# A two-layer hybrid diffusion backbone on one Trainium2 core: the start, the phase boundaries and the filler work of the mixers are rearranged

## The chip, the cores and the metric

The kernel runs on one core of a Trainium2 chip. A core has a matmul engine (TensorE, in the profile PE, with its weight loads as PEld), a vector engine (VectorE, DVE), an engine for activations and copies (ScalarE, ACT), a general one (GpSimd, POOL) and one that issues DMAs (SyncE, SP). Each works through its own instructions in order, and they wait for one another by semaphores. The metric is the device time of one execution, in microseconds (us). The kernel before took 2119.14 us in the median of three runs (2117.68 to 2120.08).

## The reference, cut to what matters

Everything is float32. There are 256 latent tokens and 256 context tokens of width 1024 and two layers. In each layer nine modulation vectors of width 1024 (shift, scale and gate for each of three sublayers) come from `silu(c)` for latent tokens and from `silu(c_ctx)` for context tokens:

```python
sc, scc = jax.nn.silu(c), jax.nn.silu(c_ctx)
for l in range(DEPTH):
    mod = (sc @ w_ada[l] + b_ada[l]).reshape(B, 1, N_MOD, D)
    mod_c = (scc @ w_ada[l] + b_ada[l]).reshape(1, 1, N_MOD, D)
    h = ffn_half_step(h, g_ffn1[l], mod[:, :, 0], mod[:, :, 1], mod[:, :, 2], ...)
    u = modulate(rmsnorm(h, g_mix[l]), mod[:, :, 3], mod[:, :, 4])
    y, yc = token_mixer(u, uc, ...)
    h = h + mod[:, :, 5] * y
    h = ffn_half_step(h, g_ffn2[l], mod[:, :, 6], mod[:, :, 7], mod[:, :, 8], ...)

def ffn_half_step(h, g, shift, scale, gate, w1, w3, w2):
    u = modulate(rmsnorm(h, g), shift, scale)
    return h + 0.5 * gate * ((jax.nn.silu(u @ w1) * (u @ w3)) @ w2)
```

The context stream goes through the same steps with `mod_c`, but not behind the mixer of the last layer. The token mixer projects u into latent attention (8 heads), a pooling mixer, a gated linear attention (GLA, 4 heads) and three sigmoid gates of width 1024. It projects each branch back to 1024, multiplies it by its gate, sums the three and applies `w_out`.

## The kernel before

**Tiles.** Activations lie transposed: 128 features on the partitions, 512 tokens on the free axis (256 latent, then 256 context), so a vector of width 1024 is eight tiles (k = 0 to 7). `self.h` is the residual in that form. Tiles of 128 x 512 come from a pool of 70 slots, PSUM tiles from a pool of eight.

**Products.** A float32 product is done as three matmuls of rounded parts (`mm3`, L238 to L240): each operand is split into a high part, written by ScalarE (`whi`, `uhi`, `hi`, L190), and a low part, the difference, written by VectorE (`wlo` on L202, `ulo` on L521 or L560).

**Weights.** `Weights` holds a list of all weight loads, written down in a first pass over the program. `run_ahead` loads the next units into four raw buffers and splits them while at most `room` slots are held. `room` is set by phase (ROOM_1 and ROOM_2 in the first FFN, ROOM_FFN, ROOM_MIX).

**Order.** The program is written as one stream. A planner then places each engine's instructions by their place in that stream (or a priority lowered by `high_priority(offset=-LATE)`) and by its own estimate of when operands are ready. `behind(i, others)` adds an order without a wait for data: i is placed after the others.

**Phases.** ffn(0,1), mixer(0), ffn(0,2), ffn(1,1), mixer(1), ffn(1,2). Behind a phase the mean of squares of the new residual is taken (`ms`, L508), `rstd` from it, then `ut`, `uhi`, `ulo`, and the next phase's products start. In the last FFN only 256 tokens are left, and its output is made by tokens: `ht` is the residual turned, `gt` the gate spread over rows.

**Modulation.** A slab (l, j) is 512 of the 9216 columns of `w_ada[l]`, in eight row blocks. Slab i = j // 2 is the half j % 2 of modulation vector i. `ada` has two forms. On TensorE (L370), a slab's eight products go to four column groups of one PSUM tile, are copied (`adaev`), turned (L384), reduced and added to the bias. The four first slabs (0, 2, 1, 3 of layer 0) are done so from rows loaded at the start, as are the two of EDGE, whose rows come over POOL's queue: (0,17) at the head of ffn(0,2) and (1,17) at the head of ffn(1,2). On VectorE, all others: per row block two multiply-adds (L401, L403), at the end two transposes, two reductions (L418, L419) and one small matmul (L424). `ada_all` is a generator over all slabs, and `adas(n)` advances it by n steps. On VectorE a step also earns half a credit. ADA holds the steps given per phase.

**Start.** `setup` loads x and ctx by tokens, then the rows of slabs 0 and 2, three units of weights, and the rows of slabs 1 and 3. ScalarE takes the squares, `xr` is x normalized, `turned` turns it into `hr`, and `residual` turns x into `h`. `first_norm` makes u from `hr`, and `dense_first` multiplies six output tiles by the k of half 0 (k below 4, slabs 0 and 2), then by those of half 1, calling one entry of `steps` after each k.

**Mixer.** `filler` yields pieces of projection work (gates, pooling inputs, GLA inputs, branch products), while `attend` and `gla` are the latency-bound chains. For each step of a chain FILL gives credit, and each whole credit advances the filler by one piece. `gate(j)` is one gate tile of 24 matmuls. While the filler waits for another chain it yields without work.

Of the kernel before, what the change touches and what calls it, by code (L numbers as in the profile page):

```python
# [15 lines left out]
P = 128  # L16
# [22 lines left out]
NHALF, NSLOT, ROOM_FFN, ROOM_MIX, RAWS = 4, 70, 20, 20, 4  # L39
RAWS_ADA = 3  # L40
ROOM_1, ROOM_2, LAST = 16, 36, 4
# [4 lines left out]
GATES = (2, 12)  # L46
EDGE = {(1, 17): (1, 2), (0, 17): (0, 2)}
# [94 lines left out]
class Net:  # L142
    def __init__(self, nc, a, cst, msk, vecs, wa2, out, pools, w, wada):
# [6 lines left out]
        self.ahead = self.seconds = None  # L150
# [83 lines left out]
    def mm3(self, out, wts, x, start, stop):  # L234

        (wh, wl), (xh, xl) = wts, x
        mm = self.nc.tensor.matmul
        mm(out, wh, xh, start=start, stop=False)  # L238
        mm(out, wh, xl, start=False, stop=False)  # L239
        mm(out, wl, xh, start=False, stop=stop)  # L240
# [12 lines left out]
    def setup(self):  # L253
# [39 lines left out]
        self.act(out=self.csil[:, :, 0:2], in_=self.vec[0][:, V_C:V_C + 16].rearrange("p (s k) -> p k s", s=2), func=AF.Silu)  # L293
# [5 lines left out]
        for j in range(4):  # L299
# [5 lines left out]
            self.act(out=f, in_=f, func=AF.Exp, scale=-0.5)  # L305
# [5 lines left out]
        self.residual(range(4), [normed])  # L311
        self.hr = []
        for k in range(KD):
            t = self.slot(name="hr")
            if k % 2:
                self.act(out=t, in_=self.turned(xr, k), func=AF.Copy)
            else:
                nc.vector.tensor_copy(t, self.turned(xr, k))
            self.hr.append(t)

    def turned(self, x, k):
        ps = self.ps()
        for j in range(4):
            self.nc.tensor.transpose(ps[:, j * P:(j + 1) * P], x[j][k // 4][:, (k % 4) * P:(k % 4 + 1) * P], self.ident)
        return ps

    def residual(self, ks, others=()):
        for k in ks:
            if k < 4:
                i = self.nc.vector.tensor_copy(self.h[:, k, :], self.turned(self.xin, k))  # L330
                if self.tc:
                    self.behind(i, others)
            else:
                self.act(out=self.h[:, k, :], in_=self.turned(self.xin, k), func=AF.Copy)
# [24 lines left out]
    def ada(self, l, j):  # L359
# [4 lines left out]
        if early or self.on_pe:  # L364
            ps = self.ps("ada")
            for u in range(4):
                for k in range(2 * u, 2 * u + 2):
                    unit = None if early else self.ada_unit(l, j, k)
                    g = k % 4
                    nc.tensor.matmul(ps[32 * g:32 * g + 32, :], self.csil[:, k, :], self.early[j][k] if early else unit.hi,  # L370
                                     start=(k < 4), stop=(k >= 4))
# [8 lines left out]
            if not early or j in (1, 3):  # L380
                yield
# [7 lines left out]
            if early:  # L389
                yield  # L390
                if j in (0, 2):
                    yield
# [1121 lines left out]
```

## Time and profile before

| what | value |
|---|---|
| median of three runs | 2119.14 us |
| the profiled execution | 2120.19 us |
| its span (first to last instruction) | 2118.4 us |
| mean granted TensorE clock | 0.994 |
| HBM read | 287.44 MB |
| DMA busy in the first 40 us (16 engines) | 1.00 |
| DMA busy from 417 to 860 us (mixer(0)) | 0.32 |

The span leaves out what lies before the first and after the last instruction, 1.8 us here. Matmuls are pipelined: the record of a product is longer than the distance to the next, so TensorE can be busy all the time and still run slower than elsewhere. A stretch row of the profile gives its limits and length, then for each engine the busy time and the number of instructions, then the share of the TensorE clock that was granted, the share of the DMA engines and GB/s. In a row of the waits stand the waiting engine and line, who ended the wait, the time in total, how often, and the longest. A row of the timeline gives start, length, engine, line, operation, tiles, count, and the idle time before it with who ended it. L190 and L202 are helpers, so their groups are told apart by tile names.

### The profile page before, as it was taken

To read this page: it belongs to the slowest core of one execution; us is meant where nothing else is said; L and a number is where in the kernel's file an instruction comes from. 1 tells how busy PE (TensorE), PEld (TensorE's weight loads), DVE (VectorE), ACT (ScalarE), POOL (GpSimd) and SP (SyncE) were. 2 spreads that over 40 slices of the span, in tenths; PEclk is the share of its full clock that TensorE was granted. 3 is DMA by queue.
4 is the path that set the end of the run, shared out by engine and by line. 5 is a ranking of instruction groups with operands and counts; after the bars stand their busy time and mean duration, and the time that the engine had idled before them with its cause. 6 is when DMAs were issued, how large, how long until landed. Compare 5 with 4: busy or idle time off the path is not lost.

```text
span 2118.4 us, 30235 instructions
## 1 busy us (share of the span) xinstructions
PE 2071.1 (98%) x11308; PEld 1738.7 (82%) x11308; DVE 1449.1 (68%) x2876; ACT 883.3 (42%) x1805; POOL 138.4 (7%) x264
## 2 busy tenths in 40 slices
PE   7999999999999999999999999999999999998999
PEld 4888888977777888788888898888888887897997
DVE  4789588875877664766965886685554688665564
ACT  5423223464445553432322343322343566654452
POOL 0011011000100000101110100010000000000000
PEclk9999999999999999999999999999999999999999
DMA  9557456424423223445744645473451343565663
GB/s 319 150 157 206 125 170 169 118 59 122 137 75 83 67 70 95 130 139 139 216 132 131 173 125 154 110 224 114 121 151 36 102 119 85 140 169 145 182 205 121
DMA packets 416836, 290.48 MB, mean 137 GB/s; under 512 B 18608, under 2 KB 388912, under 8 KB 416688
## 3 DMA queue, kind: packets, MB, share of 16 engines
q1 hardware_dynamic: 395920, 221.22, 37.0%
q0 software_dynamic: 20480, 67.13, 11.1%
q8 instruction: 89, 1.46, 0.3%
q14 instruction: 59, 0.48, 0.1%
q10 hardware_dynamic: 288, 0.20, 0.0%
HBM read 287.44 MB, written 1.05 MB: 136 GB/s over the span
## 4 chain that ended last, share of the span: by engine, by line
PE 52%; issue 41%; DMA 3%; DVE 2%; POOL 1%; ACT 0%; SPq 0%; POOLq 0%; DVEq 0%; ACTq 0%
PE ps L238 14%; PE ps L240 14%; PE ps L239 14%; DMA raw<-in_w_ada_dram 2%; PE fill L238 2%; PE fill L240 2%; PE fill L239 2%; DMA ada<-in_w_ada_dram 1%; POOL raw L355 1%; PE sc L1145 1%; DVE adaacc L403 1%; PE ada L370 1%; PE pt L1163 0%; PE av L1181 0%; DVE wlo L202 0%
## 5 line engine op out<-in xcount | busy, mean ns | idle before, releaser
L202 DVE TENSOR_TENSOR wlo<-raw,whi 128x512 fp32r<-128x512 f32 (+4 forms) x912 | 532.5, 618 | 103.3 <-ACT whi L190 92.0
L238 PE MATMUL ps<-uhi,whi 128*128 128x512 f32 (+1 forms) x1584 | 555.4, 353 | 7.8 <-ACT uhi L190 7.8
L239 PE MATMUL ps<-ulo,whi 128*128 128x512 f32 (+1 forms) x1584 | 554.8, 351 | 0.2 <-DVE ulo L560 0.2
L240 PE MATMUL ps<-uhi,wlo 128*128 128x512 f32 (+1 forms) x1584 | 554.5, 351 | 0.0
L190 ACT ACTIVATE whi<-raw 128x512 fp32r<-128x512 f32 (+4 forms) x912 | 467.7, 567 | 173.6 <-DMA raw<-in_ffn_w_dram 53.7
L238 PEld LDWEIGHTS ps<-uhi,whi 128*128 128x128 f32 x1584 | 299.6, 190 | 54.1 <-ACT uhi L190 12.0
L240 PEld LDWEIGHTS ps<-uhi,wlo 128*128 128x128 f32 x1584 | 300.7, 190 | 46.1 <-issue 5.8
L239 PEld LDWEIGHTS ps<-ulo,whi 128*128 128x128 f32 x1584 | 300.9, 190 | 40.6 <-issue 1.9
L403 DVE SCALAR_TENSOR_TENSOR adaacc<-raw,csil,adaacc 128x512 f32<-128x512 f32 x420 | 303.9, 746 | 32.7 <-DMA raw<-in_w_ada_dram 32.1
L238 PE MATMUL ps<-hi,whi 128*128 128x512 f32 (+1 forms) x738 | 271.2, 368 | 1.5 <-ACT hi L190 1.5
L240 PE MATMUL ps<-hi,wlo 128*128 128x512 f32 (+1 forms) x738 | 269.9, 366 | 0.0
L239 PE MATMUL ps<-lo,whi 128*128 128x512 f32 (+1 forms) x738 | 269.6, 366 | 0.0
L190 ACT ACTIVATE silu<-ps 128x512 f32<-128x512 f32 (+1 forms) x88 | 47.8, 543 | 495.7 <-PE ps L240 495.7
L355 POOL DMA_DIRECT2D raw<-in_w_ada_dram x256 | 137.4, 537 | 1783.2 <-DVE adaacc L401 713.7
L659 DVE TENSOR_TENSOR silu<-silu,ps 128x512 f32<-128x512 f32 (+1 forms) x88 | 54.5, 619 | 245.7 <-PE ps L240 140.0
L238 PE MATMUL fill<-uhi,whi 128*128 128x512 f32 (+1 forms) x576 | 204.2, 355 | 3.9 <-ACT whi L190 3.9
L240 PE MATMUL fill<-uhi,wlo 128*128 128x512 f32 (+1 forms) x576 | 196.7, 342 | 0.2 <-DVE wlo L202 0.2
L239 PE MATMUL fill<-ulo,whi 128*128 128x512 f32 (+1 forms) x576 | 196.2, 341 | 0.0
L238 PEld LDWEIGHTS ps<-hi,whi 128*128 128x128 f32 x738 | 139.1, 189 | 24.0 <-ACT hi L190 1.7
L239 PEld LDWEIGHTS ps<-lo,whi 128*128 128x128 f32 x738 | 139.2, 189 | 22.6 <-DVE lo L202 0.2
L240 PEld LDWEIGHTS ps<-hi,wlo 128*128 128x128 f32 x738 | 139.2, 189 | 22.6
L238 PEld LDWEIGHTS fill<-uhi,whi 128*128 128x128 f32 x576 | 110.0, 191 | 26.2 <-issue 8.5
(279 smaller groups left out, 2304.8 us busy)
## 6 DMA issues: line engine op xcount, KB each, us to landing
raw<-in_ffn_w_dram SPq DMA_DIRECT2D x192, 512.0 KB, 4.7
raw<-in_w_ada_dram POOLq DMA_DIRECT2D x256, 256.0 KB, 3.4
raw<-in_w_in_dram SPq DMA_DIRECT2D x86, 512.0 KB, 4.5
raw<-in_ffn_w_dram SPq DMA_DIRECT2D x48, 384.0 KB, 4.4
raw<-in_ffn_w_dram SPq DMA_DIRECT2D x48, 320.0 KB, 3.8
raw<-in_w_branch_dram SPq DMA_DIRECT2D x48, 256.0 KB, 2.9
ada<-in_w_ada_dram SPq DMA_DIRECT2D x32, 256.0 KB, 5.4
raw<-in_w_out_dram SPq DMA_DIRECT2D x16, 512.0 KB, 5.0
```

The lines of the kernel that those rows point to most:

```text
L190: i = self.nc.scalar.activation(**k)
L202: second = lambda: self.nc.vector.tensor_tensor(out=lo, in0=src, in1=f32hi, op=ALU.subtract)
L238: mm(out, wh, xh, start=start, stop=False)
L239: mm(out, wh, xl, start=False, stop=False)
L240: mm(out, wl, xh, start=False, stop=stop)
L355: self.nc.gpsimd.dma_start(out=t, in_=src)
L370: nc.tensor.matmul(ps[32 * g:32 * g + 32, :], self.csil[:, k, :], self.early[j][k] if early else unit.hi, start=(k < 4), stop=(k >= 4))
L403: nc.vector.scalar_tensor_tensor(out=acc[s], in0=unit.hi, scalar=c, in1=acc[s], op0=ALU.mult, op1=ALU.add)
L659: nc.vector.tensor_tensor(out=s[:, 0:n], in0=s[:, 0:n], in1=p3[:, 0:n], op=ALU.mult)
L1145: nc.tensor.matmul(sc[:, 0:nk], q[h][:, tt * P:(tt + 1) * P], keys[h][:, k0:T], start=True, stop=True)
```

## The change

- **Start.** SiLU of c is made from Exp, an add, a reciprocal and a product, where a Silu activation stood. `residual` copies even k with VectorE and odd k with ScalarE. Tiles 0 to 5 of it come ahead of the products of slab 0, tiles 6 and 7 behind `hr`. Slab 0's products are advanced inside `setup` (`adas(4)`), ahead of `hr`, and `hr`'s transposes are put behind the last of them. The products of a slab are kept in order, and those of slabs 1 and 3 behind the last product written before them. ROOM_1 goes from 16 to 12. Half 1's three units are asked for in a new entry `more`, after slab 1 is finished and before slab 3. The ScalarE operations of `first_norm` count as users of the activation table.
- **Boundaries.** EDGE is empty, so slabs (0,17) and (1,17) take their turn in `ada_all`, on VectorE.
- **Last FFN.** The turn of the residual by tokens (`ht`) moves from behind m = 4 to the head of the phase, ahead of its weight units and its norm. The gate's spread (`gt`) moves from m = 4 to m = 8.
- **Mixers.** In mixer(0), up to four gates or output gates instead of two are made while the pooled tiles are awaited. In mixer(1), up to sixteen gate tiles (0 to 7, 16 to 23) are made while attention's outputs are awaited; behind branch 0 only the missing ones are made.

```diff
-ROOM_1, ROOM_2, LAST = 16, 36, 4
+ROOM_1, ROOM_2, LAST = 12, 36, 4
-GATES = (2, 12)
-EDGE = {(1, 17): (1, 2), (0, 17): (0, 2)}
+GATES = (4, 12)
+LATER = (0, 16)
+EDGE = {}
...
-        self.act(out=self.csil[:, :, 0:2], in_=self.vec[0][:, V_C:V_C + 16].rearrange("p (s k) -> p k s", s=2), func=AF.Silu)
+        c, e = self.vec[0][:, V_C:V_C + 16], self.tiny(16, "esil")
+        self.act(out=e, in_=c, func=AF.Exp, scale=-1.0)
+        nc.vector.tensor_scalar(out=e, in0=e, scalar1=1.0, scalar2=None, op0=ALU.add)
+        nc.vector.reciprocal(out=e, in_=e)
+        by_k = lambda t: t.rearrange("p (s k) -> p k s", s=2)
+        nc.vector.tensor_tensor(out=self.csil[:, :, 0:2], in0=by_k(c), in1=by_k(e), op=ALU.mult)
...
-        self.residual(range(4), [normed])
+        self.residual(range(6), (normed, last))
+        self.adas(4)
         self.hr = []
         for k in range(KD):
             t = self.slot(name="hr")
             if k % 2:
-                self.act(out=t, in_=self.turned(xr, k), func=AF.Copy)
+                self.act(out=t, in_=self.turned(xr, k, self.products), func=AF.Copy)
...
+        self.residual(range(6, KD))
+        self.xin = None
+        self.adas(1)
...
                 for k in range(2 * u, 2 * u + 2):
+                    g = k % 4
                     unit = None if early else self.ada_unit(l, j, k)
-                    g = k % 4
-                    nc.tensor.matmul(ps[32 * g:32 * g + 32, :], self.csil[:, k, :], self.early[j][k] if early else unit.hi,
-                                     start=(k < 4), stop=(k >= 4))
+                    others = [self.last_product] if j in (1, 3) and not k else [self.products] if k else []
+                    self.products = nc.tensor.matmul(ps[32 * g:32 * g + 32, :], self.csil[:, k, :], self.early[j][k] if early else unit.hi,
+                                                     start=(k < 4), stop=(k >= 4))
+                    if early and self.tc:
+
+                        self.behind(self.products, others)
...
         if begin:
             norm = self.first_norm()
             self.adas(5)
-            self.residual(range(4, KD))
-            self.xin = None
-            self.adas(5)
...
             first[0].extend(part(0, [2]))
-            first[1].extend(part(1, [0]))
+
+            def more():
+                self.adas(1)
+                self.w.room = 2 * ROOM_1
+                first[1].extend(part(1, [0, 1, 2]))
 
             def rest():
                 self.adas(1)
                 next(norm)
                 self.w.room = ROOM_2
-                first[1].extend(part(1, [1, 2]))
+                self.w.run_ahead()
...
             self.w.room = ROOM_FFN
+            ht = self.by_tokens() if final else None
             first = unit(0) + unit(1)
...
-                        steps = [lambda: None, lambda: self.adas(4), lambda: self.adas(1), lambda: self.adas(4), rest]
+                        steps = [lambda: None, lambda: self.adas(4), more, lambda: self.adas(4), rest]
...
-        up(0, 4)
+        up(0, 8)
...
-        up(4, KF)
+        up(8, KF)
...
+        later = [gate(j) for j in (*range(8), *range(16, 24))][0:LATER[l]]
         while len(self.oa) < 4:
-            yield 1
+            if later:
+                yield from later.pop(0)
+            else:
+                yield 1
...
-        for dc in range(4):
-            yield from gate(16 + dc)
+        for dc in range(4 if self.full else 8):
+            if 16 + dc not in self.gates:
+                yield from gate(16 + dc)
```

`by_tokens` holds the sixteen transposes and four ScalarE copies of `ht` as they stood in the last FFN.

More of the change, by code (lines that the diff above doesn't have):

```diff
@@ L149, in __init__ @@
         self.have = set()
-        self.ahead = self.seconds = None
+        self.ahead = self.seconds = self.products = None
         self.after, self.owed, self.on_pe, self.edge = iter(()), 0, False, []
@@ L239, in mm3 @@
         mm(out, wh, xl, start=False, stop=False)
-        mm(out, wl, xh, start=False, stop=stop)
+        self.last_product = mm(out, wl, xh, start=False, stop=stop)
     def parts(self, src, n=T):
@@ L304, in setup @@
             self.act(out=f, in_=f, func=AF.Ln, scale=1.0 / D, bias=self.eps[:, 0:1])
-            self.act(out=f, in_=f, func=AF.Exp, scale=-0.5)
+            last = self.act(out=f, in_=f, func=AF.Exp, scale=-0.5)
             xr.append([self.slot(name="xr") for _ in range(2)])
@@ L315, in setup, with turned, residual @@
             if k % 2:
-                self.act(out=t, in_=self.turned(xr, k), func=AF.Copy)
+                self.act(out=t, in_=self.turned(xr, k, self.products), func=AF.Copy)
             else:
-                nc.vector.tensor_copy(t, self.turned(xr, k))
+                nc.vector.tensor_copy(t, self.turned(xr, k, self.products))
             self.hr.append(t)
-    def turned(self, x, k):
+        self.residual(range(6, KD))
+        self.xin = None
+        self.adas(1)
+    def turned(self, x, k, other=None):
         ps = self.ps()
         for j in range(4):
-            self.nc.tensor.transpose(ps[:, j * P:(j + 1) * P], x[j][k // 4][:, (k % 4) * P:(k % 4 + 1) * P], self.ident)
+            i = self.nc.tensor.transpose(ps[:, j * P:(j + 1) * P], x[j][k // 4][:, (k % 4) * P:(k % 4 + 1) * P], self.ident)
+            if other and self.tc:
+                self.behind(i, [other])
         return ps
-    def residual(self, ks, others=()):
+    def residual(self, ks, others=None):
         for k in ks:
[L329 to L332, printed above, removed]
-            else:
-                self.act(out=self.h[:, k, :], in_=self.turned(self.xin, k), func=AF.Copy)
+            ps = self.turned(self.xin, k)
+            if k % 2:
+                i = self.act(out=self.h[:, k, :], in_=ps, func=AF.Copy)
+            else:
+                i = self.nc.vector.tensor_copy(self.h[:, k, :], ps)
+            if self.tc and others:
+                self.behind(i, [others[k % 2]])
     def setup_rest(self):
@@ L379, in ada @@
             self.evac = self.act(out=ev, in_=ps, func=AF.Copy)
-            if not early or j in (1, 3):
-                yield
+            yield
             p2 = self.ps("ada2")
@@ L557, in first_norm @@
                     t, a, b = self.half("ut"), self.am[0][1][:, k, s:s + 1], self.mod[0][:, k, s:s + 1]
[L558 removed]
+                    self.users.append(self.act(out=hi[:, c], in_=self.hr[k][:, c], func=AF.Identity, scale=a, bias=b))
                     nc.vector.tensor_scalar(out=t, in0=self.hr[k][:, c], scalar1=a, scalar2=b, op0=ALU.mult, op1=ALU.add)
@@ L706, in ffn @@
             return
-        up(0, 4)
+        up(0, 8)
         assert {(l, 8, 0), (l, 8, 1)} <= self.have
-        ht = []
-        for j in range(2):
-            for c in range(2):
-                ps = self.ps()
-                for k in range(4):
-                    nc.tensor.transpose(ps[:, k * P:(k + 1) * P], self.h[:, 4 * c + k, j * P:(j + 1) * P], self.ident)
-                t = self.slot(name="ht")
-                self.act(out=t, in_=ps, func=AF.Copy)
-                ht.append(t)
         gt = []
@@ L753, in ffn, with by_tokens @@
         self.w.done(*us)
+    def by_tokens(self):
+        nc = self.nc
+        ht = []
+        for j in range(2):
+            for c in range(2):
+                ps = self.ps()
+                for k in range(4):
+                    nc.tensor.transpose(ps[:, k * P:(k + 1) * P], self.h[:, 4 * c + k, j * P:(j + 1) * P], self.ident)
+                t = self.slot(name="ht")
+                self.act(out=t, in_=ps, func=AF.Copy)
+                ht.append(t)
+        return ht
     def mixer(self, l):
@@ L761, in mixer @@
         self.l, self.full, self.n = l, full, n
-        self.w.room = ROOM_MIX
+        self.w.room = ROOM_MIX[l]
         def load(t):
```

5 lines of the change are left out of this document (1 added, 4 removed).

## The prediction

> **What bounds the kernel now.** I read the engine totals first, then who TensorE waited for, then equal stretches of TensorE's time side by side.
>
> ```profile
> span 2118.4 us, 30235 instructions
> PE 2071.1 (98%) x11308; PEld 1738.7 (82%) x11308; DVE 1449.1 (68%) x2876; ACT 883.3 (42%) x1805; POOL 138.4 (7%) x264
> PE ada L370 <- DMA raw<-in_w_ada_dram: 4.1, 2, 3.2
> PE fill L238 <- ACT whi L190: 3.9, 1, 3.9
> PE ms L508 <- DVE acc L492: 3.7, 1, 3.7
> PE rq L1131 <- ACT rq L190: 3.2, 1, 3.2
> 1814.00:1905.00 91.00, 90.95 (x756) 90.66 (x756) 61.15 (x121) 56.26 (x121) 0.00 (x0) 1.00 0.65 175
> ```
>
> TensorE is busy 98% of the span and VectorE 68%, so TensorE's order is the clock of this kernel, and a gain can only come from matmuls taken off it, from its waits, or from its slow stretches. The waits are a handful, each with its place. The last row (a stretch: length, then busy time and count of PE, PEld, DVE, ACT, POOL, then granted clock) gives the price of a 256-wide product: 91 us for 756, 0.120 us each, from start to start. Busy time hides slow stretches, so I count matmuls per stretch.
>
> **The two phase boundaries.** EDGE put one modulation slab on TensorE at the head of ffn(0,2) and one at the head of ffn(1,2). The first is compared with the same 18.9 us behind the next boundary of the same width, which has no slab.
>
> ```profile
> 871.10:890.00 18.90, 15.67 (x77) 9.92 (x78) 10.88 (x30) 7.93 (x17) 4.27 (x8) 0.82 0.36 111
> 1248.80:1267.70 18.90, 18.81 (x155) 18.76 (x156) 12.97 (x35) 8.79 (x19) 0.00 (x0) 1.00 0.01 2
> L370 PE MATMUL ada<-raw,csil 128*32 128x512 f32 x10 | 5.9, 879 | 3.2 <-DMA raw<-in_w_ada_dram 3.2
> 1913.50:1945.60 32.10, 31.05 (x206) 25.84 (x207) 15.51 (x33) 12.47 (x28) 2.07 (x4) 0.89 0.41 115
> L370 PE MATMUL ada<-raw,csil 128*32 128x512 f32 x10 | 5.1, 700 | 1.0 <-DMA raw<-in_w_ada_dram 1.0
> L384 PE MATMUL ada<-cst,adaev 128*128 128x128 f32 x4 | 0.6, 272 | 0.0
> 1905.70:1913.60 7.90, 3.18 (x13) 0.66 (x11) 6.05 (x14) 5.55 (x11) 0.70 (x2) 0.78 1.01 270
> 1910.20:1913.50 3.30, 2.42 (x8) 0.20 (x6) 1.82 (x5) 2.64 (x5) 0.60 (x2) 0.50 1.02 275
> 1913.60:1916.90 3.30, 2.34 (x10) 2.04 (x11) 3.16 (x8) 2.50 (x6) 0.89 (x2) 0.50 0.90 281
> 1917.00:1920.30 3.30, 3.30 (x10) 1.41 (x10) 1.91 (x5) 0.51 (x1) 0.54 (x1) 0.50 0.05 21
> ```
>
> First boundary: 77 matmuls less 10 of the slab and 2 of the mean leave 65 products, where the plain boundary did 153: 88 short, 88 x 0.120 = 10.6 us. That is slab products, a 3.2 us wait for their rows, and a clock of 0.82. What remains, the wait for uhi before the stretch, both boundaries have. **Gain 10.6, bounds 9 to 11.**
>
> Second boundary: 206 less 14 leave 192 products, worth 23.1 us, in 32.1: 9.0 us lost. Not all returns. The clock is at half in three slices, and the first follows TensorE's wait for the last column's square sum, which stays. Without the slab the stretch of 7.9 us ahead of the first product is emptier still, so I leave one slice of about 3.4 us at half clock: 1.7 us. **Gain 7.3, bounds 5 to 9.**
>
> [...]
>
> The slabs move to VectorE, at the end of its list.
>
> ```profile
> L403 DVE SCALAR_TENSOR_TENSOR adaacc<-raw,csil,adaacc x420: 706/745/754, 85.3 to 1503.9; 128x512 f32<-128x512 f32 x140
> L401 DVE TENSOR_SCALAR adaacc<-raw,csil x60: 442/482/513, 84.5 to 1488.9; 128x512 f32<-128x512 f32 x60
> L418 DVE STREAM_TRANSPOSE adaacc<-adaacc x60: 664/702/711, 101.1 to 1507.0; 128x512 f32<-128x512 f32 x60
> L419 DVE TENSOR_REDUCE adapart<-adaacc x60: 639/674/689, 102.9 to 1507.7; 128x16 f32<-128x512 f32 x60
> 1550.00:1613.20 63.20, 63.20 (x343) 55.04 (x341) 32.51 (x79) 25.70 (x64) 0.00 (x0) 1.00 0.47 124
> ```
>
> A slab is 14 x 0.745 + 2 x 0.482 + 2 x 0.702 + 2 x 0.674 = 14.1 us of VectorE; its 8 loads on POOL's queue move with it, none is added. The list ended at 1508 us. Two more slabs, 28 us, go behind it, where VectorE is idle 30.7 of 63.2 us and TensorE never; credits left over run into mixer(1), which has ten. Slab (1,17) is first read in the last FFN, behind that. **Cost 0, up to 2** if a step falls into the boundary chain at 1613.
>
> **The tokens of the residual.** by_tokens moves 16 transposes and 4 copies from inside the last FFN to its head.
>
> ```profile
> 1945.70 1.91 PE L715 MATMUL ps<-cst,h 128*128 128x128 f32 x16
> 1910.80 0.47 ACT L190 ACTIVATE rstd<-ms,eps 128x256 f32<-128x256 f32 x1 [1.28 <-PE ms L508]
> L190 ACT ACTIVATE ht<-ps x4: 577/592/607, 1946.8 to 1948.2; 128x512 f32<-128x512 f32 x4
> ```
>
> TensorE saves 1.9 us in its dense stretch, since the 7.9 us gap above has room for them. But the copies (4 x 0.59) stand in ScalarE's in-order queue ahead of rstd, uhi and the eight whi, and ScalarE has 1.28 us idle there. Two fit; the others can delay uhi, and so the first product, by up to 1.2, or 2.4 if none fits. I take 0.6. **Gain 1.3, bounds -0.5 to 1.9.** The diagonal products behind m = 8 keep their own cost.
>
> **The start.**
>
> ```profile
> 15.00 5.40 DMA ada<-in_w_ada_dram
> 15.44 1.28 ACT L186 ACT_TABLE_LOAD   x1
> 16.38 2.47 DVE L330 COPY h<-ps 128x512 f32<-128x512 f32 x4
> 22.69 0.65 PE L384 MATMUL ada<-cst,adaev 128*128 128x128 f32 x4 [0.80 <-ACT adaev L190]
> 23.18 1.91 PE L324 MATMUL ps<-cst,x 128*128 128x128 f32 x16
> 25.02 1.92 PE L370 MATMUL ada<-ada,csil 128*32 128x512 f32 x16
> 30.21 0.73 PE L238 MATMUL ps<-uhi,whi 128*128 128x512 f32 x2 [1.81 <-ACT uhi L190]
> 23.92 11.54 SPq L274 DMA_DIRECT2D ada<-in_w_ada_dram x16
> 37.17 0.34 SPq L345 DMA_DIRECT2D cst<-in_cst_dram x1
> 41.52 4.48 SPq L229 DMA_DIRECT2D raw<-in_ffn_w_dram x4
> 41.45 0.63 ACT L190 ACTIVATE whi<-raw 128x512 fp32r<-128x512 f32 x1 [6.26 <-DMA raw<-in_ffn_w_dram]
> 30.20:54.60 24.40, 23.15 (x112) 14.89 (x113) 13.26 (x36) 10.49 (x21) 0.00 (x0) 1.00 0.91 288
> ```
>
> In the chain of waits the last scale row has landed at 20.4, yet its slab starts at 25.0: in TensorE's queue stood the turn of slab 0 and 16 residual transposes. Slab to first product takes 30.21 - 25.02 = 5.2. With slab 0 run as its rows land and the residual turned earlier, slab 2 can start at 20.4: first product at 25.6; if its rows are used as they land, only the last pair is late, near 23.9. I take 25, 5.2 early. The change orders more by hand, and what it queues is this. On TensorE hr's transposes stand behind slab 0's last product, whose row lands near 15 by the same chain; xr is whole only when the h copies start, at 16.4, so nothing is lost. On VectorE and ScalarE three copies of h each now stand behind xr and the last Exp, and hr's copies behind these; VectorE's four took 2.47 us and end far ahead of the first uhi. Six PSUM tiles instead of four wait for them, of eight, so hr's turn starts with one free: some tenths of a us in a stretch that waits for rows anyway. The Exp form of SiLU saves a switch of tables (1.28 us) and adds three small VectorE operations, both under the row loads: 0.
>
> What is late next is DMA, at 0.91 share over the 24.4 us of half 0 (its 112 records are 72 products and 40 of slabs 1 and 3). The last rows of slab 3 are issued at 35.5 and, with the same 5.4, land near 41; half 0 would end near 49, so these rows fit. ROOM_1 at 12 takes half 1's first unit out of ScalarE's queue ahead of slab 1's copy, where it waited 6.26 us for DMA: worth up to 1, not counted. The two last units of half 1 are issued at 41.5 to 46.0 behind the constants and land some 5 later, but would be needed by 52; if that order stays, an us may be given back, and if the earlier conversions free their buffers first, nothing. **Gain 5, bounds 0 to 7.5.**
>
> **The two mixers.**
>
> ```profile
> 488.00:498.00 10.00, 6.82 (x27) 4.21 (x27) 6.91 (x14) 7.39 (x13) 0.00 (x0) 0.83 0.35 96
> 1777.00:1814.00 37.00, 32.74 (x266) 21.24 (x265) 30.38 (x82) 22.87 (x56) 0.00 (x0) 1.00 0.10 29
> L202 DVE TENSOR_TENSOR wlo<-raw,whi 128x512 fp32r<-128x512 f32 x7 | 4.5, 681 | 0.0
> ```
>
> Mixer(0), GATES 2 to 4: TensorE stands 3.2 us before turning rq, with 0.83 of the clock over 10 us (1.7 us more). Its filler is then out of work until the fourth pooled tile. A gate is 24 products of twice the width, 24 x 0.24 = 5.8 us, more than the wait. It also brings 2 whi and 2 wlo ahead of ScalarE's and VectorE's backlog, which lengthens the wait but not past the gate. **Gain 3.5, bounds -1 to 4.9.**
>
> Mixer(1), LATER 16: in the 37 us while attention is awaited TensorE is idle 4.3, VectorE 6.6. A gate there is 24 x 0.120 = 2.9 us of TensorE against 2 x 0.68 = 1.4 of VectorE, so it fills more than it delays. The gates are then missing where branch 0 hides its parts of oa: about 1 us. **Gain 3, bounds -1 to 4.3.**
>
> **Sum.** 10.6 + 7.3 + 1.3 + 5 + 3.5 + 3 = 30.7 us. The profiled execution took 2120.2 (span 2118.4), 1.0 above the median of 2119.1; taken from the median, 2088.4, which I round to 2089.
>
> **Rivals.**
> - *The start is bound by DMA* (chance 0.17): rows and units keep their landing times, the early products only wait longer before half 1. Gain there 0: 2094. For: the share of 0.91. Against: the slab starts 4.6 us after its rows.
> - *Only the boundaries pay* (0.15): the order in the queues puts gates and first slab where TensorE was busy anyway, so the change does not do what it says there. 10.6 + 7.3 + 1.3: 2100. For: the waits for rq and for whi both end with ScalarE, which an early gate loads further.
> - *More is recovered* (0.10): no half-clock slice, half 0 without its 1.2 us of idle (24.4 less 23.2), both mixers dense (1.4 and 1.3), and 1 for the copy of slab 1: 6.6 more, 2082.
> - *Slower* (0.05): sixteen gate tiles hold 8 of the 70 slots through attention, so that conversions wait for a slot and TensorE for whi, as once now for 3.9 us. It decides from nine such waits among the sixteen gates: 9 x 3.9 = 35 us against 30.7 gained, 2123. Against: there is one such wait in the trace now, with 12 gates kept early.
>
> The forecast holds 0.53. The range of 2080 to 2104 takes in the first three rivals with the unknown costs and leaves out 2 in 10. About 0.2% is what a measurement of this kernel can tell from no change: faster 0.92, same 0.03, slower 0.05.
>
> **What would show it.** L370 loses the slabs' 32 records and L403 rises from 420 to 448, the last after 1504 us. The 18.9 us behind the first boundary hold about 153 products at clock 1.00. The first product stands near 25 us, the second half's start near 49. No idle of 3 us stands ahead of L1131; gates are written between 1740 and 1815 in mixer(1). I am wrong if ScalarE's copies of ht stand between ms and rstd, if new waits for whi appear in mixer(1), or if the unit loads of half 1 still land after 51.

## The result and the profile after

| | before | changed |
|---|---|---|
| median of four runs each | 2118.74 us (2117.68 to 2120.08) | 2094.16 us (2093.27 to 2096.24) |
| the profiled execution | 2120.19 us | 2093.27 us |
| its span | 2118.4 us | 2091.5 us |
| mean granted TensorE clock | 0.994 | 0.996 |

The ratio is 0.9885, with a 95% interval of 0.9868 to 0.9902: 24.6 us less. The two profiled executions lie 26.9 us apart, since the one of before took longer than each of the four timed runs and the one of the changed kernel was the fastest of its four. What follows divides these 26.9 us.

The changed kernel's page, its span, engine totals and the group of the slabs on VectorE (line, engine, operation, tiles, count, then busy time and mean ns):

```profile
span 2091.5 us, 30190 instructions
PE 2053.2 (98%) x11272; PEld 1735.6 (83%) x11272; DVE 1475.9 (71%) x2923; ACT 881.1 (42%) x1802; POOL 138.9 (7%) x264
L417 DVE SCALAR_TENSOR_TENSOR adaacc<-raw,csil,adaacc 128x512 f32<-128x512 f32 x448 | 325.1, 747 | 36.0 <-DMA raw<-in_w_ada_dram 35.0
```

The changed code shifts line numbers: a product is L239 to L241 (L238 to L240 before), a slab's products on TensorE are L384 (L370), its turn is L400 (L384), the multiply-add on VectorE is L417 (L403), and the helper for ScalarE is L191 (L190). TensorE is as busy in percent as before and has 36 matmuls less. VectorE has the two slabs more: 448 multiply-adds instead of 420.

Who TensorE waited for in the changed kernel (total us, times, longest), and stretches of it in the order of the rows shown of before:

```profile
PE ps L239 <- ACT uhi L191: 11.6, 6, 3.8
PE fill L239 <- ACT whi L191: 3.9, 1, 3.9
PE ada L400 <- ACT adaev L191: 3.6, 2, 2.8
PE ps L735 <- DVE dg L734: 1.9, 1, 1.9
```

```profile
866.40:885.30 18.90, 18.88 (x156) 18.83 (x156) 12.90 (x35) 8.75 (x18) 0.00 (x0) 1.00 0.01 2
1885.50:1893.60 8.10, 2.98 (x22) 2.10 (x20) 5.15 (x11) 7.09 (x14) 0.00 (x0) 0.89 0.91 235
1893.60:1898.60 5.00, 5.00 (x23) 5.00 (x24) 4.86 (x13) 3.10 (x7) 0.00 (x0) 0.50 0.32 95
484.00:494.00 10.00, 10.00 (x48) 6.10 (x47) 7.93 (x16) 4.65 (x9) 0.00 (x0) 1.00 0.37 105
1760.00:1798.00 38.00, 36.63 (x337) 31.13 (x335) 33.11 (x77) 25.01 (x58) 0.00 (x0) 1.00 0.46 122
```

The waits for slab rows, for rq and for the square sum are gone. The wait for whi has stayed, and three have come or grown: for uhi (3.8 in one place), for adaev (2.8 in one place) and for dg. A smaller one (1.2, for h) stands ahead of the last transposes of ht. Behind the first boundary stand 154 products (156 less 2 of the mean) at full clock, where 65 stood. Around rq's turn in mixer(0) TensorE is never idle. In mixer(1), while attention is awaited, 1.4 us of 38 are idle instead of 4.3 of 37.

**Where the 26.9 us came from.** Both traces hold 9918 recorded products, and at the ends of the phases the n-th of one is the n-th of the other. The start of the same product in both traces tells how far the changed kernel is ahead there:

| product | place | before, us | changed, us | ahead | gained in the part | forecast |
|---|---|---|---|---|---|---|
| 0 | first of the kernel | 30.21 | 28.69 | 1.52 | | |
| 53 | last ahead of slab 3's turn | 49.95 | 46.94 | 3.01 | | |
| 54 | first behind it; half 1 starts 18 products later | 50.53 | 50.55 | -0.02 | | |
| 150 | first FFN, dense | 72.70 | 72.43 | 0.27 | start 0.3 | 5 |
| 3000 | late in mixer(0) | 782.59 | 777.87 | 4.72 | mixer(0) 4.5 | 3.5 |
| 3650 | behind the first boundary | 913.34 | 897.53 | 15.81 | boundary 11.1 | 10.6 |
| 7350 | late in ffn(1,1) | 1692.78 | 1677.21 | 15.57 | slabs on VectorE -0.2 | 0 |
| 8590 | end of mixer(1) | 1904.94 | 1884.67 | 20.27 | mixer(1) 4.7 | 3 |
| 9000 | last FFN, dense | 1975.23 | 1948.30 | 26.92 | second boundary with ht and gt 6.65 | 7.3 + 1.3 |

The other parts came within 2 us of their terms. The start did not: it gave 0.3 instead of 5. Its rows say where the early products went. First TensorE, then SyncE's DMA issues, then ScalarE of the changed kernel:

```profile
12.95 5.67 PE L384 MATMUL ada<-ada,csil 128*32 128x512 f32 x16
18.55 3.71 PE L334 MATMUL ps<-cst,xr 128*128 128x128 f32 x32
23.51 1.92 PE L384 MATMUL ada<-ada,csil 128*32 128x512 f32 x16
...
28.69 1.22 PE L239 MATMUL ps<-uhi,whi 128*128 128x512 f32 x2 [1.81 <-ACT uhi L191]
...
43.80 1.92 PE L384 MATMUL ada<-ada,csil 128*32 128x512 f32 x16
...
50.13 0.66 PE L400 MATMUL ada<-cst,adaev 128*128 128x128 f32 x4 [2.81 <-ACT adaev L191]
```

```profile
6.09 11.79 SPq L275 DMA_DIRECT2D ada<-in_w_ada_dram  x16
...
23.78 11.12 SPq L275 DMA_DIRECT2D ada<-in_w_ada_dram  x16
35.25 1.06 SPq L230 DMA_DIRECT2D raw<-in_ffn_w_dram  x2
36.60 0.34 SPq L358 DMA_DIRECT2D cst<-in_cst_dram  x1
37.28 0.34 SPq L358 DMA_DIRECT2D msk<-in_msk_dram  x1
37.96 2.54 SPq L358 DMA_DIRECT2D wa<-in_wa_dram  x4
41.10 4.51 SPq L230 DMA_DIRECT2D raw<-in_ffn_w_dram  x4
```

```profile
46.39 0.63 ACT L191 ACTIVATE whi<-raw 128x512 fp32r<-128x512 f32 x1 [3.87 <-DMA raw<-in_ffn_w_dram]
47.25 0.63 ACT L191 ACTIVATE whi<-raw 128x512 fp32r<-128x512 f32 x1 [0.23 <-DMA raw<-in_ffn_w_dram]
48.14 0.63 ACT L191 ACTIVATE whi<-raw 128x512 fp32r<-128x512 f32 x1 [0.26 <-DMA raw<-in_ffn_w_dram]
48.97 0.63 ACT L191 ACTIVATE whi<-raw 128x512 fp32r<-128x512 f32 x1 [0.19 <-DMA raw<-in_ffn_w_dram]
49.50 0.58 ACT L191 ACTIVATE adaev<-ada 128x512 f32<-128x512 f32 x1
```

Sixteen products of slab 0 take 5.67 us instead of 1.92: they run as their rows land, until 18.6. Behind them hr's turn (3.71) fills TensorE, and slab 2 starts at 23.5, not at 20.4. It could not have been done much earlier: the last of the sixteen loads of slabs 0 and 2 is issued near 17.5, and with the 5.4 us that these loads take in the median it lands near 23. Slab 3's products are done at 45.7. Their copy adaev stands in ScalarE's queue behind four conversions that wait for units of half 1. These units were issued from 41.1 on, behind six loads of constants. So the copy comes at 49.5, and TensorE, 3.0 us ahead until then, waits 2.81 and has lost all of it.

### The profile page after: what moved, and what is told of

Its sections match the earlier page's. It is cut to its first block, busy times and chain, and to the rows that moved or that the text cites. A ratio compares the mean times of both kernels' runs of the same rounds, so it can differ in the third digit from the quotient of the medians.

```text
span 2091.5 us, 30190 instructions
## 1 busy us (share of the span) xinstructions
PE 2053.2 (98%) x11272; PEld 1735.6 (83%) x11272; DVE 1475.9 (71%) x2923; ACT 881.1 (42%) x1802; POOL 138.9 (7%) x264
## 4 chain that ended last, share of the span: by engine, by line
PE 94%; DMA 2%; ACT 2%; DVE 1%; SPq 0%; issue 0%; DVEq 0%; ACTq 0%
PE ps L239 24%; PE ps L241 23%; PE ps L240 23%; PE fill L239 5%; PE fill L241 4%; PE fill L240 4%; PE sc L1171 2%; DMA ada<-in_w_ada_dram 1%; PE av L1207 1%; PE gv L239 1%; PE pt L1189 1%; PE gv L241 1%; PE gv L240 1%; PE o L1393 1%; ACT whi L191 0%; PE A L1352 0%
## 5 line engine op out<-in xcount | busy, mean ns | idle before, releaser
L239 PE MATMUL ps<-uhi,whi 128*128 128x512 f32 (+1 forms) x1584 | 555.5, 353 | 11.6 <-ACT uhi L191 11.6
L240 PE MATMUL ps<-ulo,whi 128*128 128x512 f32 (+1 forms) x1584 | 555.0, 351 | 0.0
L241 PE MATMUL ps<-uhi,wlo 128*128 128x512 f32 (+1 forms) x1584 | 554.3, 351 | 0.0
L191 ACT ACTIVATE whi<-raw 128x512 fp32r<-128x512 f32 (+4 forms) x912 | 467.6, 567 | 162.5 <-DMA raw<-in_ffn_w_dram 51.3
L417 DVE SCALAR_TENSOR_TENSOR adaacc<-raw,csil,adaacc 128x512 f32<-128x512 f32 x448 | 325.1, 747 | 36.0 <-DMA raw<-in_w_ada_dram 35.0
L239 PEld LDWEIGHTS ps<-uhi,whi 128*128 128x128 f32 x1584 | 300.0, 190 | 53.4 <-ACT uhi L191 12.9
L241 PEld LDWEIGHTS ps<-uhi,wlo 128*128 128x128 f32 x1584 | 301.1, 190 | 39.8 <-DVE wlo L203 0.6
L240 PEld LDWEIGHTS ps<-ulo,whi 128*128 128x128 f32 x1584 | 301.3, 190 | 39.0 <-DVE ulo L574 0.4
L239 PE MATMUL ps<-hi,whi 128*128 128x512 f32 (+1 forms) x738 | 271.3, 368 | 1.5 <-ACT hi L191 1.5
L241 PE MATMUL ps<-hi,wlo 128*128 128x512 f32 (+1 forms) x738 | 269.9, 366 | 0.0
L240 PE MATMUL ps<-lo,whi 128*128 128x512 f32 (+1 forms) x738 | 269.6, 366 | 0.0
L191 ACT ACTIVATE silu<-ps 128x512 f32<-128x512 f32 (+1 forms) x88 | 47.9, 544 | 493.5 <-PE ps L241 493.4
L239 PE MATMUL fill<-uhi,whi 128*128 128x512 f32 (+1 forms) x576 | 206.8, 359 | 3.9 <-ACT whi L191 3.9
L241 PE MATMUL fill<-uhi,wlo 128*128 128x512 f32 (+1 forms) x576 | 196.8, 342 | 0.0
L240 PE MATMUL fill<-ulo,whi 128*128 128x512 f32 (+1 forms) x576 | 196.3, 341 | 0.0
L239 PEld LDWEIGHTS ps<-hi,whi 128*128 128x128 f32 x738 | 139.1, 189 | 24.0 <-ACT hi L191 1.7
L240 PEld LDWEIGHTS ps<-lo,whi 128*128 128x128 f32 x738 | 139.2, 189 | 22.6 <-DVE lo L203 0.2
L241 PEld LDWEIGHTS ps<-hi,wlo 128*128 128x128 f32 x738 | 139.2, 189 | 22.6
L239 PEld LDWEIGHTS fill<-uhi,whi 128*128 128x128 f32 x576 | 110.0, 191 | 29.5 <-issue 10.8
```

Source lines behind the costliest of these rows:

```text
L191: i = self.nc.scalar.activation(**k)
L241: self.last_product = mm(out, wl, xh, start=False, stop=stop)
L417: nc.vector.scalar_tensor_tensor(out=acc[s], in0=unit.hi, scalar=c, in1=acc[s], op0=ALU.mult, op1=ALU.add)
```

## The experiments

Each run is the changed kernel with one edit, unless it says otherwise. None of the edits leaves work out. Times are medians of four to six runs, ratios stand to runs of the kernel before on the same chip. Differences by product are against the changed kernel's trace. Each text on record names its theories and what they give.

**The start as before** (the start's code taken back whole, the rest as changed):

```diff
-ROOM_1, ROOM_2, LAST = 12, 36, 4
+ROOM_1, ROOM_2, LAST = 16, 36, 4
...
-        self.residual(range(6), (normed, last))
-        self.adas(4)
+        self.residual(range(4), [normed])
...
+            self.residual(range(4, KD))
+            self.adas(5)
...
-                        steps = [lambda: None, lambda: self.adas(4), more, lambda: self.adas(4), rest]
+                        steps = [lambda: None, lambda: self.adas(4), lambda: self.adas(1), lambda: self.adas(4), rest]
```

> The changed kernel with the start of before (SiLU, residual, slab order, ROOM_1, units of half 1), the rest of the change kept. Theory A (the start gives back what it gains: its first product is 1.5 us earlier, but product 150 only 0.3): span 2091.8, time within 1 us of the changed kernel's 2094.2. Rival B (the start is worth its 1.5 us or more, and something later hides it in my count): 2095.7 or more, and the lag of 1.5 is still there behind product 150.

2093.70 us, ratio 0.9885 (0.9870 to 0.9899), the same as the changed kernel. The first product comes 1.24 us later, product 150 0.28 later, the end 0.24 earlier. The start's rearrangement is worth nothing as it stands, and the other parts give the whole result without it.

**The slabs back at the boundaries:**

```diff
-EDGE = {}
+EDGE = {(1, 17): (1, 2), (0, 17): (0, 2)}
```

> The changed kernel with EDGE as before: both slabs again on TensorE at the two phase heads. Theory A (the boundaries carry most of the gain): first boundary +11.1 us, second +6 to +8, time 2111 to 2113, half clock behind both. Rival B (VectorE's 28 us of extra slabs cost something elsewhere that this gives back): less than +15 in total, and products between the boundaries earlier than in the changed kernel by some us before they lose it.

2110.24 us, ratio 0.9964 (0.9952 to 0.9977). The waits of TensorE in this run:

```profile
PE ada L384 <- DMA raw<-in_w_ada_dram: 7.6, 2, 4.5
```

The trace falls back by 11.05 us at the first boundary (0.29 to 11.34 between products 2150 and 3650) and by 5.5 at the second (10.41 to 15.92 between 8590 and 9000), with less than a us in all between them. That is less than theory A's 6 to 8 at the second: behind that boundary this trace has 3.4 us at half clock, where the trace of before has 10.2. So the boundaries are worth some 16 us of the 26.9, and VectorE takes the slabs for nearly nothing. In the changed kernel their last multiply-add starts at 1572.6, long ahead of the boundary that the prediction feared for (near 1613 before the change, some 16 us earlier behind it).

**Two gates early in mixer(0), not four:**

```diff
-GATES = (4, 12)
+GATES = (2, 12)
```

> The changed kernel with GATES[0] = 2. Theory A (two more gates cover TensorE's wait for rq and keep its clock): idle of about 3.2 us ahead of the turn of rq returns with one half-clock window, +4.5 us, 2098.7, nothing else moves. Rival B (the gain in mixer(0) comes from another order of the pooling and branch work): under +2.

2098.66 us, ratio 0.9913 (0.9899 to 0.9928). TensorE waits for rq again and loses 3.1 us in mixer(0) (2.60 behind at product 2050, 5.74 at 2600). The other 2.6 us were lost at the start, in code that the edit doesn't touch: the wait for slab 3's copy was 3.2 us in this run and was followed by a slice at half clock (0.50 from 50.9 to 54.3). More on that below. So the time agrees with theory A's 2098.7 by luck: the wait came back, but no slice at half clock came with it.

**No gates while attention is awaited in mixer(1):**

```diff
-LATER = (0, 16)
+LATER = (0, 0)
```

> The changed kernel with LATER[1] = 0: no gates while attention is awaited in mixer(1). Theory A (the gates fill TensorE's idle while it waits for VectorE): +4.5 us, 2098.7, idle of about 4 us in the 37 us of the last attention steps, as before. Rival B (gates held early take slots and cause the 3.9 us wait for whi at 1681): that wait goes and the cost is under +2.

2100.46 us, ratio 0.9918 (0.9903 to 0.9933). This run's stretch beside the one of the changed kernel above:

```profile
1760.00:1798.00 38.00, 33.72 (x278) 22.77 (x278) 31.91 (x86) 24.32 (x58) 0.00 (x0) 1.00 0.10 28
```

It is idle 4.3 us, as before the change, and mixer(1) falls back by 4.8 (0.50 behind at product 7700, 5.29 at 8590). A further 1.7 were lost in the last FFN, which the edit doesn't touch: here the wait for dg, 1.9 us as in the changed kernel, was followed by 3.4 us at half clock (from 1950.7), and there it was not. The rival that feared waits for whi falls: the one of 3.9 us stands in this run, in the changed kernel and before, and there is no other.

**Half 1's units asked for behind slab 3's copy.** If the copy only stood in the wrong place in ScalarE's queue, moving the requests should free it.

```diff
-                self.w.room = 2 * ROOM_1
-                first[1].extend(part(1, [0, 1, 2]))
+                self.w.room = 16
+                first[1].extend(part(1, [0]))
...
-                self.w.run_ahead()
+                first[1].extend(part(1, [1, 2]))
```

> The changed kernel's start, but only one unit of half 1 asked for in `more` and two in `rest`, so that slab 3's copy stands ahead of these two units' whi in ScalarE's queue. Theory A (the start's gain is lost because that copy waits behind whi, and whi for the units' DMA): the copy moves from 49.5 to about 46, TensorE's 3 us ahead of the slab's turn go, product 150 comes 2 to 3 us earlier, span 2089. Rival B (the start is bound by the bytes that DMA has to bring, whatever the order): product 150 within 0.5 us of the changed kernel.

2092.80 us, ratio 0.9879 (0.9864 to 0.9894): no difference that these runs can tell. The profiled run says more. A stretch of it, early in half 0:

```profile
31.60:35.00 3.40, 3.40 (x10) 2.62 (x9) 3.40 (x10) 2.59 (x6) 0.00 (x0) 0.50 1.06 387
```

At half clock its products fell 2.11 us behind those of the changed kernel, up to slab 3's, which came at 45.91 instead of 43.80. The copy followed at once, at 47.98, the wait of 2.8 us did not occur, and product 54 was 0.92 ahead (0.54 at product 150). So a copy ahead of the conversions does take that wait away, and 3.0 us were won back in that place. What it is worth with the clock of the other run, and whether the later units would then be late, this run leaves open.

**The constants behind half 1's units** in SyncE's queue, with the rest of the start as changed:

```diff
                     for i in loads or ():
-                        self.net.behind(i, [self.net.last])
+                        self.net.behind(i, [self.net.last]); self.net.unit = i
...
-                self.behind(i, [self.last])
+                self.behind(i, [self.unit])
```

> The changed kernel with the constants of the mixers put behind the last unit of half 1 in SP's queue, ScalarE's order unchanged. Theory A and rival B both expect the two units to land about 4 us earlier (1.2 MB less ahead of them); A expects the copy of slab 3 with them, near 45.5, and product 150 2 to 3 us earlier; if neither the rows of slab 3 nor the units are what half 1 waits for, nothing changes.

2090.39 us, ratio 0.9870 (0.9856 to 0.9885). SyncE and then ScalarE in this run:

```profile
36.16 5.50 SPq L230 DMA_DIRECT2D raw<-in_ffn_w_dram  x6
41.70 0.82 SPq L358 DMA_DIRECT2D cst<-in_cst_dram  x1
```

```profile
46.06 0.63 ACT L191 ACTIVATE whi<-raw 128x512 fp32r<-128x512 f32 x1 [0.20 <-DMA raw<-in_ffn_w_dram]
46.59 0.58 ACT L191 ACTIVATE adaev<-ada 128x512 f32<-128x512 f32 x1
```

The copy still stands behind six conversions, but their loads are issued by 41.7 and it comes at 46.6, 2.9 earlier. Product 150 is 2.50 earlier and the end 2.86. The 0.4 between them came near 1690, in code that the edit doesn't touch, where this trace has one slice at half clock and the changed kernel's two (1683.6 to 1690.5). So the wait ahead of half 1 can be taken away from either end: by a copy ahead of the conversions, or by loads that no longer stand behind constants. With the latter the start gives 2.8 (0.3 and 2.5), over half of what its term had promised.

**Slab 2 ahead of hr's turn**, together with the constants later. If its rows are there at 20.4, as the prediction read, this brings the first product further forward.

```diff
-        self.hr = []
+        self.hr, first = [], self.products
+        self.adas(5)
...
+            if k == 1:
+                self.adas(1)
```

> The changed kernel with the constants behind half 1's units, and slab 2's products and copy ahead of the turn of hr. Theory A (with the units in time TensorE is dense from the first product on, so an earlier first product now counts in full): first product near 25.9 instead of 28.9, product 150 another 1.5 to 3 us earlier than with the constants alone, 2088. Rival B (the rows of slab 3 land near 41, and now they are the limit): product 150 within 0.7 us of the kernel with the constants alone, 2090.4.

2093.65 us, ratio 0.9884 (0.9867 to 0.9900): about 3 us slower than with the constants alone by the medians, from different chips, with intervals that overlap. By the traces product 150 comes 1.45 us later. TensorE in this run:

```profile
20.13 4.18 PE L386 MATMUL ada<-ada,csil 128*32 128x512 f32 x16
24.24 1.09 PE L336 MATMUL ps<-cst,xr 128*128 128x128 f32 x8
...
31.57 0.73 PE L239 MATMUL ps<-uhi,whi 128*128 128x512 f32 x2 [2.31 <-ACT uhi L191]
```

Sixteen products that take 1.92 us when their rows lie ready take 4.18, at full clock: the rows of slab 2 land until about 23.2 (the last is issued near 17.8, with 5.4 to landing), not 20.4. TensorE stood in them while hr's turn, ready, was queued behind, and the first product came at 31.6 instead of 28.7.

**The residual's turn and the gate's spread back at m = 4:**

```diff
-            ht = self.by_tokens() if final else None
...
-        up(0, 8)
+        up(0, 4)
         assert {(l, 8, 0), (l, 8, 1)} <= self.have
+        ht = self.by_tokens()
...
-        up(8, KF)
+        up(4, KF)
```

> The changed kernel with the turn of the residual and the gate's spread behind m = 4 again. Theory A (the 16 transposes are worth 1.9 us in the gap, but they covered the wait for dg, which is now 1.9, and ScalarE's copies delay the first product by 0.3): 1.9 us more of transposes, 1.3 us less of waiting for dg, first product 0.3 earlier: +0.3 in all, within noise. Rival B (the move is worth its 1.9 us): +1.5 to +2.

2094.58 us, ratio 0.9889 (0.9872 to 0.9905): the same. By products the part from mixer(1) into the last FFN loses 0.66 us (1.14 behind at product 8590, 1.80 at 9000), while the start of this run, in code that the edit doesn't touch, lost 1.9, most of it in stretches at a lower clock (0.76 from 31.6 to 35.0 and 0.59 from 50.9 to 54.3, where the changed kernel has 1.00). So this move is worth about 0.5 us, not 1.3: 0.2 of the 0.66 are lost in the slices at half clock behind the boundary. With the transposes at m = 4 the wait for dg is 0.6 us. In the changed kernel it is 1.89, since the transposes that had covered it are gone.

**The spread in the gap, too.** I tried to use the idle time at the second boundary for the gate's spread, first by making its diagonals (dg) behind the norm:

```diff
-            ht = self.by_tokens() if final else None
             first = unit(0) + unit(1)
             u, rest = self.norm_go(l, i, n)
+            if final:
+                ht, gt = self.by_tokens(), self.by_rows(self.am[l][i + 2])
```

`by_rows` holds the spread as it stood at m = 8.

> The changed kernel with both the turn of the residual and the gate's spread written behind the norm's first chunk at the head of the last FFN, so that rstd and uhi stand ahead of their copies and the spread's four products fall into TensorE's wait for uhi. Theory A (the gap has 4 us of TensorE to give away): the 2.0 us of products and the 1.9 us of waiting for dg behind m = 8 go, first product unchanged: -3 to -4 us, 2090.5. Rival B (their VectorE and ScalarE work delays the norm chain as much): within 1 us of the changed kernel.

2098.03 us, ratio 0.9906 (0.9891 to 0.9920). The waits of TensorE in this run:

```profile
PE ps L759 <- DVE dg L758: 5.6, 1, 5.6
PE ms L522 <- DVE acc L506: 4.6, 1, 4.6
```

VectorE made dg behind all the ulo, and the spread's products stood in TensorE's queue ahead of the phase's: 0.45 us ahead of the changed kernel's trace at the end of mixer(1), the run is 8.6 behind it past the boundary, and 3.9 are given back at m = 8. Neither theory had this; the place in VectorE's order decided, not the idle time.

So **the diagonals were made earlier**, in mixer(1) ahead of its last output products, with only the spread's products behind the norm and ht at the head as changed:

```diff
+            gt = self.spread() if final else None
...
-        up(0, 8)
...
-        up(8, KF)
+        up(0, KF)
...
+        if not full:
+            self.diagonals(self.am[l][8])
         out([0, 1, 2, 3])
```

> The changed kernel with the gate's diagonals made by VectorE ahead of mixer(1)'s last products, and the spread's four products and two copies written behind the norm's first chunk, so that they fall into TensorE's wait for uhi; the turn of the residual stays at the head. Theory A (what made the earlier attempt slow was dg standing behind ulo in VectorE's queue, not the products): the 2.0 us of products and the 2.2 us of waiting go from behind m = 8, the first product stays: -3.5 to -4.2 us against the changed kernel, 2090.3. Rival B (any work in that gap delays the first product by its own length): within 1 us of the changed kernel.

2089.45 us, ratio 0.9864 (0.9849 to 0.9878). TensorE's timeline and a stretch of this run:

```profile
1889.82 1.88 PE L762 MATMUL ps<-dg,ones 128*128 128x512 f32 x4
```

```profile
1895.00:1898.40 3.40, 3.40 (x18) 3.40 (x17) 3.29 (x9) 2.17 (x5) 0.00 (x0) 0.50 0.17 51
```

The spread's 1.88 us lie in the gap. The first product of the last FFN stands 8.84 us behind mixer(1)'s last one, against 8.08 in the changed kernel, but not because of the spread: from the square of the last column of h to the first uhi ScalarE takes 4.92 us in both traces, and it is this last column that came later. One slice at half clock follows the gap in this run and two in the changed kernel's, so the lead past the boundary is again the 0.52 us of the end of mixer(1). At m = 8 the wait for dg and the four products go: 3.86 us.

**All three together** (constants, slab 2, diagonals) and then **without slab 2**:

> Both together: constants behind the units, slab 2 ahead of hr, diagonals early and the spread in the gap. Theory A: the parts lie in different stretches and add up, 2094.2 less 2.7 less 1.5 to 3 less 3.5 to 4.2: 2084 to 2087. Rival B (half-clock windows fall anew with each shift, 1.7 us each): up to 2 us off that sum, either way.

2088.48 us (2086.50 to 2090.39), ratio 0.9857 (0.9843 to 0.9872): the diagonals add to the constants. Slab 2 again brings the first product late (31.66, 29.52 in the next run), but product 150 only by 0.5 us.

> The changed kernel with the constants behind half 1's units and the diagonals early, spread in the gap; slab 2 where the change has it. Theory A (slab 2 ahead of hr cost 1.5 us because its rows land only near 23.5, and TensorE stood in front of them with hr's turn behind): first product back near 29, product 150 2.5 us earlier than in the changed kernel, span about 1.5 us under the version with all three, 2083, time near 2087. Rival B (the 1.5 us were a half-clock window or spread between runs): span 2084.7 within 0.5.

2086.18 us (2085.27 to 2087.53), ratio 0.9847 (0.9833 to 0.9860): 8 us below the changed kernel, by the edits of the constants and of the diagonals. That they add up so well (2.86 and 4.38 by products, 7.42 together) is luck. In this trace product 150 was 1.5 us early, not 2.5, so the sizes at the start stay uncertain by about a us from run to run. In its place 2.2 us were won behind the second boundary, where this trace has no slice at half clock at all (1.00 from 1892.0 to 1898.6), with the same code there as in the run with the diagonals alone, which has one. Only the 3.86 us at m = 8 are the same in each run with the diagonals early.

## Why the prediction was right, and where it was not

The time came 5 us above the forecast, inside the range. By the profiled executions the changed kernel was forecast at 2120.2 - 30.7 = 2089.5 and took 2093.3. The sum is nearer than its terms: the start fell short by 4.7 and the second boundary with ht by 2, and the mixers and the first boundary gave 3.2 more than forecast. That these offset each other is luck.

- **First boundary, 10.6.** Right: 11.1 by products, 11.05 by the run that puts the slabs back, and 154 products at full clock where about 153 were named.
- **Slabs on VectorE, 0.** Right: 0.2, below what I would separate.
- **mixer(0), 3.5 and mixer(1), 3.** Right in mechanism, low in size: 4.5 and 4.7. In mixer(0) the wait for rq and the half-clock slice behind it both went, close to the upper bound of 4.9. That slice was a matter of luck, as the run with two gates shows: without it the gates were worth 3.1. In mixer(1) I took 1 us off for gates missing behind branch 0, and no such loss showed. The 4.7 lie above the upper bound of 4.3, which was TensorE's idle time. Idle time fell by 2.9 only; the rest was time in which TensorE counted as busy and yet did less (266 matmuls in 32.7 us of busy time before, 337 in 36.6 after).
- **Second boundary, 7.3, and ht, 1.3.** 6.65 together, in bounds and low by 2. The rows of the changed kernel, TensorE and then ScalarE:

```profile
1889.04 0.70 PE L522 MATMUL ms<-acc,cst 128*128 128x256 f32 x2
1893.59 1.01 PE L239 MATMUL ps<-uhi,whi 128*128 128x256 f32 x3 [3.85 <-ACT uhi L191]
...
1944.33 1.99 PE L735 MATMUL ps<-dg,ones 128*128 128x512 f32 x4 [1.89 <-DVE dg L734]
```

```profile
1888.44 1.57 ACT L191 ACTIVATE ht<-ps 128x512 f32<-128x512 f32 x3
1889.89 0.64 ACT L191 ACTIVATE whi<-raw 128x512 fp32r<-128x512 f32 x1
1890.41 0.49 ACT L191 ACTIVATE rstd<-ms,eps 128x256 f32<-128x256 f32 x1
```

The copies of ht end 0.27 us behind ms, so they cost little: the first product stands 8.08 us behind mixer(1)'s last one, 7.81 before. What I had missed is the wait for dg at m = 8 (1.89 against 0.6): with the transposes gone from there, nothing lies above it. And the 5 us of products at half clock (1893.6 to 1898.6) cost 2.5, where I had left 1.7. At the start of the kernel, transposes came to run at full clock with no other matmul ahead of them. In the last run TensorE did nothing but transposes up to 13.7 us:

```profile
7.37 2.81 PE L334 MATMUL ps<-cst,x 128*128 128x128 f32 x12
11.18 0.88 PE L334 MATMUL ps<-cst,x 128*128 128x128 f32 x6 [0.99 <-DMA x<-in_ctx_dram]
```

The first twelve took 421 ns each in the median, the others 273. Sixteen transposes at a granted clock of 0.50 (1890.9 to 1894.3 us, in the run with the diagonals behind the norm) also took 421, and sixteen at 1.00 (23.2 to 24.8 us, in the trace of before) took 272. So full clock was there with nothing but transposes run before it. In the traces of before and of the old start it also came (at 19.1 and 17.2 us; of before, from 421 ns a transpose to 273) ahead of any other matmul (19.97 and 19.69). The half clock behind the gap (0.50 from 1891.84 to 1898.67) begins inside TensorE's wait of 3.85 us for uhi. What brings it on is not shown.

- **Start, 5.** This step failed: 0.3. The prediction took "the last scale row has landed at 20.4" from one row of the chain, the one of 15.00 and 5.40. That chain follows releases: the load issued at 15.00 is the twelfth of the sixteen of slabs 0 and 2, and its landing let SyncE issue the next load of weights, at 20.42. SyncE's own row in the trace of before shows the last one issued only shortly before 18.04:

```profile
6.01 12.03 SPq L274 DMA_DIRECT2D ada<-in_w_ada_dram  x16
```

With 5.4 us more, slab 2's last row is there near 23.1, and slab 0's, read near 15, lands later too: its products ran until 18.6. In the run with slab 2 first, its products run with their rows until 24.3. The second half of the step failed as well. I wrote that DMA is late next and let the units of half 1 cost "an us" if the order behind the constants stayed. It stayed, and cost all of the 3 us that half 0 had gained, by way of slab 3's copy in ScalarE's queue. The prediction had seen slab 1's copy wait there behind a unit, and didn't ask the same of slab 3's. The rival that the start is bound by DMA, at 2094, described the outcome, down to early products that only wait longer ahead of half 1. Its reason holds in part. The rows of slab 2 do set when the first product can come. The wait ahead of half 1 was made by two orders, SyncE's issues and ScalarE's queue: changing either took it away.

Of the signs named ahead, those of the boundaries and of L1131 came, and in mixer(1) ten gates were written between 1740 and 1815 where two had been. Those against it did not come: no new wait for whi, the last conversion of half 1 starts at 48.97, and only the last 0.27 us of ht's copies lie behind ms. The first product at 25 and half 1 at 49 did not come either: the first stood at 28.7, the second (product 72) at 54.75, against 54.72 before.

## What to carry to other kernels

Work moved forward is worth only what the next late operand lets through: follow the moved work to the next operand that is loaded, and look at what stands ahead of its load in the issuing queue and ahead of its copy in the copying engine's. A landing in the chain of waits says when something was released; when the last row of a tile is there is shown by the issue of its last load and the time to landing, or by work that runs through all its rows. And when work is taken from a place, look for the short wait that it was hiding.

## What the runs showed of the hardware

The price of a short idle time is not fixed. Before the change, TensorE's wait for rq was followed by a slice at half clock. In the run with two gates the same wait, as long to 0.01 us, was not. First the kernel before, timeline and stretch, then the run with two gates:

```profile
494.02 1.12 PE L1131 MATMUL rq<-cst,rq 128*128 128x128 f32 x4 [3.18 <-ACT rq L190]
```

```profile
493.60:497.00 3.40, 2.98 (x9) 2.58 (x10) 1.86 (x4) 3.37 (x6) 0.00 (x0) 0.50 0.45 112
```

```profile
496.39 0.66 PE L1157 MATMUL rq<-cst,rq 128*128 128x128 f32 x4 [3.19 <-ACT rq L191]
```

```profile
496.30:499.70 3.40, 3.31 (x17) 2.82 (x18) 1.64 (x4) 3.37 (x6) 0.00 (x0) 1.00 0.58 149
```

The slices at half clock in the trace of before begin at 493.6, 875.9, 1701.9 and 1910.1 us and last 3.4, 6.8, 3.4 and 10.2 us, at 0.50 of the clock. The wait of 3.2 us for rq was followed by a slice of 3.4 us at half clock, worth up to 1.7 us by my estimate (half its length), in one trace and by none in the other, and what decides between the two is not shown. The wait of 1.9 us for dg was followed by such a slice in the run without early gates in mixer(1) (0.50 from 1950.7 to 1954.1) and by none in the changed kernel (1.00 from 1944.3 to 1947.7). Slices at half clock are also where most of the 2.11 us of the run with the units behind the copy come from, and part of the 2.6 at the start of the run with two gates. A difference of a us or two between two traces is an edit's only after the slices at half clock have been compared.
